# A hybrid decoder layer on one core: DeltaNet values turned in place by VectorE, outputs normed chunk by chunk and turned in halves

## The chip, the cores and the metric

The kernel runs on one NeuronCore of a Trainium2 chip. The core has TensorE (PE, matrix products, whose weight loads are listed as PEld), VectorE (DVE), ScalarE (ACT), GpSimd (POOL) and SyncE (SP), which here issues nearly all of the transfers; 16 DMA engines carry them. The engines run side by side, each through its own queue in order, and wait for each other by semaphores. The metric is the time of one execution on the device in microseconds; smaller is better.

## The reference, cut to what matters

The whole is one decoder layer for 1024 tokens of width 1024. One input projection feeds two mixers: a gated DeltaNet (4 heads of 128) and a dilated attention (8 heads of 64). Their outputs go through one output projection, a gated MLP of width 2816 with a short convolution follows, and a final norm. The change lies in the DeltaNet's values and outputs:

```python
qkv_a = silu(causal_dwconv(qkv_a, conv_qkv_w))       # width 4, per channel
qa = l2norm(qa) * 128**-0.5; ka = l2norm(ka)         # va as it is
# per chunk of 64 tokens: a triangular solve, then
def step(state, xs):
    uv, wk, qd, at, ke, ge = xs
    u = uv - wk @ state                              # uv comes from the values va
    o = qd @ state + at @ u
    state = ge * state + ke.T @ u
    return state, o
o_a = rmsnorm(o_a, gdn_norm_w) * silu(z)             # norm over the 128 features of a head
x = x + concat([o_a, o_b]) @ w_out
```

The kernel works with chunks of 128 tokens, of which there are eight (`NCH`).

## The kernel before, in words

Activations lie by feature: 128 features on the partitions, 1024 tokens along the free dimension. Weights and activations of the large products are split in a high and a low part (`split`: ACT makes the high part, DVE the remainder), and each product is three matrix products (`mm3`).

*Who sets the order.* The program is written as Python generators (streams) which a small planner, `Weave`, interleaves. It keeps a model time for PE and for the other engines (`Engine.account`: a fixed cost and a cost per element) and lets a stream go on when its tiles should be ready (`need`, with a slack in us that is added). The streams have levels: the recurrence (`chain`) goes ahead of the dense products (`dense`). The order that comes out is PE's order for good: every matrix product gets an order token. On the other engines a scheduler of the language orders the instructions by a simulated timeline and by priority; `uv` and `ua` are DVE and ACT with high priority, `ve` and `ac` without, `po_` is POOL, `sy` and `sq_` are transfers on SP's queue. `after(a, b)` puts a behind b on their engine. Line 140 is the call through which the instructions of normal priority go, line 142 the same for high priority, 193 a matrix product, 197 a transpose on PE and 202 a half-height one.

*The dense products.* `DENSE` lists 128-column blocks of the input projection in order: the last keys, two of the attention's blocks, then queries and values of heads 0 to 3 in turn, then the rest of the attention's blocks and the gates z. The first key blocks are made before. For each block `dense` splits the next weights (`wk`, `weight`) and fetches the ones after (`raw_weight`, tile `wst`); `conv_silu` makes the convolution on ACT and DVE, and the SiLU on ACT.

*Preparation of a head.* `kprep` turns keys to token order (`tokens`: eight PE transposes into PSUM, copied out by ACT), and makes decays and the matrices `um`. `qprep` does the queries and parks them in DRAM (`qpark`, `atpark`). `vprep` turns the values: eight PE transposes, and ACT copies each 128 x 128 block out of PSUM, scaled per token by `nk`, into `vtok`. After the last key, `forward_sub` inverts all 32 x 32 diagonal blocks on DVE in 31 steps; the result goes through DRAM (`xdram`, `xtdram`) and `merges` joins the blocks on PE to the inverse, in `um`. That 32 x 32 turning trick is also used for the attention's values: DVE turns each 32 x 32 block of a tile, and the transfers through DRAM (`avdram`) put the blocks in place.

*The recurrence.* `chain(h)`, one stream per head, waits until all merges and all values are done. Per chunk: two products with the state, `r` on DVE, a product with the inverse, `wke` on DVE and its copy `w` on ACT, the new state `ct` on DVE; then the output chunk, which replaces the value chunk in `vtok` (ACT, then DVE), and its sum of squares (`osq`, ACT, accumulated in a column of `ms`). Heads 2 and 3 run some chunks behind heads 0 and 1. PE fills its waits with dense products.

*The output of a head.* After the eighth chunk DVE makes mean plus EPS in `ms`, POOL raises all eight columns to the power -1/2 (`rsqrt`) and multiplies the whole `vtok` by them. `finish` then turns `vtok` back on DVE in four instructions of 128 x 256 (tile `ft`) and writes it to `mixer`. `dense` reads it back when it makes the gate z (tile `og`), again with the blocks put in place by the transfer. The tag of a tile names the ring of slots that it takes; `ft` takes one of the key slots.

Attention begins after the recurrence; its softmax uses ACT's Exp. The SiLU before and the Exp after lie in different function tables, so ACT loads a table in between.

## Time and profile before

| | |
|---|---|
| median of 3 runs | 1201.64 us (1201.17 to 1201.66) |
| the profiled execution | 1199.71 us, its span 1197.9 us |
| granted TensorE clock, mean | 0.998 |
| instructions | 18219 |
| PE busy | 1184.3 us, 99% |
| DVE / ACT / POOL busy | 967.5 / 566.4 / 54.3 us |

The profile is one execution. "Busy" counts the time in which an engine has at least one instruction under way. A group line gives line, engine, operation, output and inputs, shape and count, then busy time and mean nanoseconds of one instruction, then the idle time just before them and what ended it. A timeline line starts with start and duration in us; in brackets stands the idle time before it and who released it. `SPq` is a transfer's issue on SP's queue; the landing of the data is told apart. Spans on POOL are rough, and ends of matrix products are modelled, so that neighbours overlap in the list.

### The profile page before, as it was taken

How to read it: one execution, taken by the hardware profiler on the slowest of the kernel's cores; microseconds unless marked ns; L12 is line 12 of the kernel's file. 1: busy time of each engine (PE TensorE's matmuls, PEld its weight loads, DVE VectorE, ACT ScalarE, POOL GpSimd, SP SyncE). 2: the span in 40 equal slices, each digit the busy share in tenths (PEclk: the TensorE clock that was granted, in tenths of full speed). 3: DMA queues.
4: the chain of work that ended last, by engine and by line, in shares of the span. 5: the costliest groups of instructions: out<-in, count | busy, mean ns of one | idle time of the engine just before them, and what ended most of it. 6: DMA issues, size and time to landing. Idle time of an engine off the chain costs nothing.

```text
span 1197.9 us, 18219 instructions
## 1 busy us (share of the span) xinstructions
PE 1184.3 (99%) x6994; PEld 979.5 (82%) x6994; DVE 967.5 (81%) x1552; ACT 566.4 (47%) x1113; POOL 54.3 (5%) x50
## 2 busy tenths in 40 slices
PE   9999999998999999999999999999999999999997
PEld 7888888897777777888888888888888888888887
DVE  7686985586766687777898888989888889898987
ACT  7383344363433344555454544445444453445452
POOL 0212110023000000000000000000000000000001
PEclk9999999999999999999999999999999999999999
DMA  7423235536643314443222223131222396356724
GB/s 237 106 75 103 78 118 131 150 114 189 185 100 128 98 37 142 148 158 106 77 70 99 88 71 106 53 106 59 100 89 69 105 378 211 119 181 218 240 99 155
DMA packets 98600, 152.72 MB, mean 127 GB/s; under 512 B 37936, under 2 KB 51024, under 8 KB 98512
## 3 DMA queue, kind: packets, MB, share of 16 engines
q1 hardware_dynamic: 97792, 151.02, 39.4%
q8 instruction: 55, 0.90, 0.3%
q10 hardware_dynamic: 720, 0.53, 0.1%
q14 instruction: 33, 0.27, 0.1%
HBM read 115.59 MB, written 35.93 MB: 126 GB/s over the span
## 4 chain that ended last, share of the span: by engine, by line
PE 95%; DVE 2%; ACT 1%; issue 1%; DMA 1%; POOL 0%; DVEq 0%; ACTq 0%; POOLq 0%
PE ps L193 46%; PE pa L193 20%; PE dw L193 17%; PE pc L193 10%; PE ps L197 1%; PE ps L202 1%; DMA wst<-in_wu 1%; ACT sm L142 0%; PE warm L193 0%; DVE x1h L140 0%; DVE sm L142 0%; DVE aqkv L140 0%; DVE T L140 0%; ACT L142 0%; DVE wst L140 0%
## 5 line engine op out<-in xcount | busy, mean ns | idle before, releaser
L193 PE MATMUL dw<-pr 128*128 128x512 f32 (+1 forms) x984 | 211.4, 376 | 0.0
L193 PEld LDWEIGHTS dw<-pr 128*128 128x128 f32 x984 | 176.7, 188 | 33.7
L193 PE MATMUL ps<-xhi,whi 128*128 128x512 f32 x448 | 184.4, 412 | 0.0
L193 PE MATMUL ps<-xhi,wlo 128*128 128x512 f32 x448 | 175.2, 391 | 0.0
L193 PE MATMUL ps<-xlo,whi 128*128 128x512 f32 x448 | 174.8, 390 | 0.0
L193 PE MATMUL pa<-T,pair 128*128 128x512 f32 x528 | 127.1, 390 | 0.5 <-ACT u L140 0.5
L193 PEld LDWEIGHTS pa<-T,pair 128*128 128x128 f32 x528 | 98.9, 188 | 21.5 <-ACT u L140 1.0
L193 PEld LDWEIGHTS ps<-xhi,whi 128*128 128x128 f32 x448 | 84.3, 188 | 19.3 <-issue 2.7
L193 PEld LDWEIGHTS ps<-xhi,wlo 128*128 128x128 f32 x448 | 84.1, 188 | 18.5
L193 PEld LDWEIGHTS ps<-xlo,whi 128*128 128x128 f32 x448 | 84.4, 188 | 14.3
L140 ACT ACTIVATE u<-pa 128x512 f32<-128x512 f32 x44 | 26.3, 598 | 109.7 <-PE pa L193 109.7
L140 DVE SCALAR_TENSOR_TENSOR y<-xu,fcw,y 128x1023 f32<-128x1023 f32 (+1 forms) x44 | 56.4, 1281 | 24.4 <-ACT y L140 24.4
L140 ACT ACTIVATE whi<-wst 128x1024 fp32r<-128x1024 f32 (+2 forms) x38 | 38.5, 1014 | 68.8 <-PE ps L193 61.6
L140 ACT ACTIVATE pr<-wd 128x1024 fp32r<-128x1024 f32 x33 | 35.0, 1061 | 74.6 <-DVE wd L140 37.2
L193 PE MATMUL pa<-B,A 128*128 128x512 f32 x264 | 63.5, 389 | 0.0
L193 PE MATMUL pa<-T,S 128*128 128x512 f32 x264 | 63.4, 389 | 0.0
L193 PE MATMUL pc<-T,S 128*128 128x512 f32 x264 | 63.4, 389 | 0.0
L193 PE MATMUL pc<-B,pair 128*128 128x512 f32 x264 | 63.4, 389 | 0.0
L140 DVE TENSOR_TENSOR wst<-wst 128x512 f32<-128x512 f32 x88 | 60.4, 686 | 0.8
L193 PE MATMUL ps<-B,pair 128*128 128x512 f32 x252 | 60.5, 389 | 0.0
L142 ACT ACTIVATE sm<-sm,mx 128x128 f32<-128x128 f32 (+7 forms) x64 | 35.5, 555 | 50.3 <-DVE mx L142 50.3
L193 PEld LDWEIGHTS pc<-T,S 128*128 128x128 f32 x264 | 49.5, 188 | 10.3
(242 smaller groups left out, 2234.2 us busy)
## 6 DMA issues: line engine op xcount, KB each, us to landing
wst<-in_wu SPq DMA_DIRECT2D x44, 512.0 KB, 3.6
wd<-in_wd SPq DMA_DIRECT2D x44, 512.0 KB, 4.5
wst<-in_wi SPq DMA_DIRECT2D x25, 512.0 KB, 3.6
upark<-y SPq DMA_DIRECT2D x22, 512.0 KB, 3.5
r<-upark SPq DMA_DIRECT2D x22, 512.0 KB, 10.1
wa<-in_wd SPq DMA_DIRECT2D x22, 256.0 KB, 2.9
apark<-aqkv SPq DMA_DIRECT2D x8, 512.0 KB, 2.7
wst<-in_wo SPq DMA_DIRECT2D x8, 512.0 KB, 3.8
```

Of the source, the lines that this page charges most:

```text
L140: return getattr(eng, op)(*a, **kw)
L142: return getattr(eng, op)(*a, **kw)
L193: tc.stamp_issue_order_token(nc.tensor.matmul(dst, lhs, rhs, start=start, stop=stop, **kw).ins, TOKEN)
L197: tc.stamp_issue_order_token(nc.tensor.transpose(dst, src, ident).ins, TOKEN)
L202: tc.stamp_issue_order_token(nc.tensor.transpose(dst, src[rows], ident[rows, rows]).ins, TOKEN)
```

## The change

Five things change.

1. `vprep` makes no PE transposes any more. DVE turns the 32 x 32 blocks of the values' tile in place, four strided transfers write it to a new DRAM buffer `vdram`, one reads it back in token order as `vtok`, and ACT scales its eight blocks from SBUF. The planner waits for the tile with slack `VSLACK`, 3 us; the slack before the turning is 1 us instead of 3.
2. The output is normed by chunk: the square carries the factor 1/128 by its scale, POOL adds EPS and raises one column, and one chunk later ACT scales the chunk (`normed`).
3. The output is turned and written in halves (`half_turned`): the first four chunks at the fifth chunk of the recurrence, the others at the end. The halves take slots of the ring `t2`, which the planner charges to DVE by hand.
4. The weights of three blocks (`CHAINED`) are split in two halves of 512 columns.
5. After the last head's values ACT runs one Exp on a tile of one column (`mark`), ordered behind that head's SiLU.

```diff
+VSLACK = 3.0
+CHAINED = [("a", 1, 1), ("a", 1, 2), ("a", 2, 0)]
...
-    def weight(src, n=1024, st=None):
+    def weight(src, n=1024, st=None, parts=1):
...
-        lows_made.append(split(st, hi, lo))
+        for i in range(parts):
+            sl = slice(i * n // parts, (i + 1) * n // parts)
+            low = split(st[:, sl], hi[:, sl], lo[:, sl])
+        lows_made.append(low)
...
+    vdram = dp.tile([H, P, S], F32, name="vdram")
...
         if j // 4 != 1:
-            ac.activation(y, y, AF.Silu)
+            last["silu"] = ac.activation(y, y, AF.Silu)
...
-                nxt = wk(None, raw.pop())
+                nxt = wk(None, raw.pop(), 1 + (DENSE[i + 1] in CHAINED))
...
                 v = conv_silu(xr, 8 + h, "vT", "qa")
+                if h == H - 1:
+                    after(ac.activation(mark, mhalf[:, :1], AF.Exp), last["silu"], "the table changes once")
                 wv.add(4, vprep(h, v))
...
     def vprep(h, vT):
         yield from wv.until(("q", h))
-        yield wv.need(vT, slack=SLACK)
-        G[h]["vtok"] = yield from tokens(vT, A("vtok", ("dv", "dw")[h % 2]), G[h]["nk"])
+        yield wv.need(vT, slack=1.0)
+        vtok, nk = A("vtok", ("dv", "dw")[h % 2]), G[h]["nk"]
+        ve.transpose(vT, vT)
+        blocks = vdram[h].rearrange("(a t) (c b i) -> b t c a i", a=4, c=NCH, b=4)
+        for b in range(4):
+            sq_.dma_start(blocks[b], vT[32 * b:32 * b + 32].rearrange("t (c a i) -> t c a i", c=NCH, a=4))
+        sy.dma_start(vtok, vdram[h])
+        yield wv.need(vtok, slack=VSLACK)
+        for c in range(NCH):
+            cs = slice(c * P, (c + 1) * P)
+            ac.activation(vtok[:, cs], vtok[:, cs], AF.Copy, scale=nk[:, c:c + 1])
+        G[h]["vtok"] = vtok
         wv.done.add(("v", h))
...
-            ua.activation(osq, vtok[:, cs], AF.Square, accum_out=ms[:, c:c + 1])
+            ua.activation(osq, vtok[:, cs], AF.Square, scale=128.0 ** -0.5, accum_out=ms[:, c:c + 1])
+            po_.tensor_scalar(ms[:, c:c + 1], ms[:, c:c + 1], EPS, None, op0=OP.add)
+            rsqrt(ms[:, c:c + 1], ms[:, c:c + 1], 1)
+            if c:
+                normed(vtok, ms, c - 1)
+            if c == 4:
+                half_turned(h, vtok, 0)
             wv.done.add(("c", h, c))
 
-        uv.tensor_scalar(ms, ms, 1.0 / 128, EPS, op0=OP.mult, op1=OP.add)
-        rsqrt(ms, ms, NCH)
-        po_.tensor_tensor(v8(vtok), v8(vtok), ms[:, :, None].to_broadcast([P, NCH, P]), op=OP.mult)
-        wv.add(1, finish(h, vtok))
-
-    def finish(h, osb):
-        yield wv.need(osb, slack=FSLACK)
-        t = A("ft", "kT*")
-        by_feature, src = ...
-        for b in range(4):
-            ve.transpose(by_feature[:, b], src[:, b])
-            yield 0.4
-        sy.dma_start(mixer[h], t)
+        wv.add(1, finish(h, vtok, ms))
+
+    def normed(osb, ms, c):
+        cs = slice(c * P, (c + 1) * P)
+        wv.free["scalar"] = max(wv.free["scalar"], wv.pe) + 0.23
+        nc.scalar.activation(osb[:, cs], osb[:, cs], AF.Copy, scale=ms[:, c:c + 1])
+
+    def half_turned(h, osb, hh):
+        t = tile_(sp, [P, 512], F32, "ft", "t2", 2)
+        by_feature = t.rearrange("p (b c i) -> p c b i", b=4, c=4)
+        src = osb[:, half(hh)].rearrange("p (c b j) -> p c b j", c=4, b=4)
+        for c in (0, 2):
+            wv.free["vector"] = max(wv.free["vector"], wv.pe) + 0.34
+            nc.vector.transpose(by_feature[:, c:c + 2], src[:, c:c + 2])
+        sy.dma_start(mixer[h].rearrange("p (b c i) -> p b c i", b=4, c=NCH)[:, :, 4 * hh:4 * hh + 4],
+                     t.rearrange("p (b c i) -> p b c i", b=4, c=4))
+
+    def finish(h, osb, ms):
+        yield wv.need(ms, slack=FSLACK)
+        normed(osb, ms, NCH - 1)
+        half_turned(h, osb, 1)
         wv.done.add(("o", h))
```

5 lines of the change are left out of this document (2 added, 3 removed).

## The prediction

> **What bounds the kernel now.** I read the page's first part, the chain's shares, PE's waits, and then a table of stages.
>
> ```profile
> PE 1184.3 (99%) x6994; PEld 979.5 (82%) x6994; DVE 967.5 (81%) x1552; ACT 566.4 (47%) x1113; POOL 54.3 (5%) x50
> PE 95%; DVE 2%; ACT 1%; issue 1%; DMA 1%; POOL 0%; DVEq 0%; ACTq 0%; POOLq 0%
> PE ps L193 <- DVE ct L142: 1.6, 2, 1.2
> PE ps L193 <- ACT w L142: 1.4, 2, 1.0
> PE ps L202 <- DVE sm L142: 1.1, 1, 1.1
> 115.00:175.00 60.00, 60.00 (x306) 50.83 (x306) 55.22 (x122) 24.12 (x72) 8.10 (x3) 1.00 0.26 88
> 175.00:198.00 23.00, 23.00 (x119) 19.32 (x117) 14.19 (x22) 10.39 (x30) 4.50 (x3) 1.00 0.69 181
> 198.00:226.00 28.00, 28.00 (x522) 24.36 (x522) 12.11 (x17) 8.68 (x22) 0.36 (x2) 1.00 0.48 141
> 226.00:292.00 66.00, 62.95 (x419) 56.62 (x418) 47.76 (x136) 33.53 (x130) 12.43 (x10) 1.00 0.42 134
> 292.00:470.00 178.00, 176.53 (x1791) 135.67 (x1790) 129.15 (x345) 71.23 (x213) 7.15 (x10) 1.00 0.41 114
> ```
>
> TensorE carries 95% of the chain. The stage rows give the stretch, then busy time of PE, PEld, DVE, ACT and POOL, then clock, DMA share and GB/s. From 115 to 226 us, where the values are made, PE is never idle: what leaves PE there shortens the kernel, unless a wait takes its place. In the recurrence (226 to 292) PE idles 3.05 us, and to 470 another 1.47; waits can be won there, 4.5 us at most.
>
> **Part 1: 32 transposes leave TensorE.**
>
> ```profile
> L197 PE MATMUL ps<-ident,vT 128*128 128x128 f32 x32 | 4.2, 274 | 0.0
> 127.31 1.04 PE L197 MATMUL ps<-ident,vT 128*128 128x128 f32 x8
> 128.10 0.47 PE L193 MATMUL ps<-xhi,whi 128*128 128x512 f32 x1
> 128.42 0.39 PE L193 MATMUL ps<-xlo,whi 128*128 128x512 f32 x1
> 128.65 0.40 PE L193 MATMUL ps<-xhi,wlo 128*128 128x512 f32 x1
> ```
>
> Eight transposes of one head hold PE from 127.31 to 128.10, 0.79 us; the product behind them takes a step of 0.32 where the next takes 0.23. So 0.88 us a head, 3.5 us for four (bounds: 4 x 0.79 = 3.2, and the group's 4.2). I take **-3.5**.
>
> **Part 2: the detour of the values.** Per head it adds one DVE transpose, four strided writes and one read on SP's queue, and ACT scales from SBUF instead of PSUM. Nearest rows: the attention's own values take the same way (`avt`, `avdram`).
>
> ```profile
> L140 DVE STREAM_TRANSPOSE avt<-aqkv x4: 1245/1245/1246, 209.9 to 393.8; 128x1024 f32<-128x1024 f32 x4
> L140 SPq DMA_DIRECT2D avdram<-avt x16: 580/676/1854, 212.4 to 397.1; - x16
> DMA to landing us min/median/max: 2.7/3.4/4.9
> qT<-apark SPq DMA_DIRECT2D x4, 512.0 KB, 4.0
> 128.61 2.15 ACT L142 ACTIVATE vtok<-ps,nk 128x128 f32<-128x128 f32 x8
> 232.24 0.31 ACT L142 ACTIVATE osq<-vtok 128x128 f32<-128x128 f32 x1
> 196.99 1.06 ACT L140 ACTIVATE vT<-vT 128x1024 f32<-128x1024 f32 x1 [3.65 <-DVE vT L140]
> 225.53 1.05 PE L193 MATMUL ps<-vtok,um 128*128 128x128 f32 x8
> ```
>
> The last head decides. Its SiLU ends at 198.05; transpose 1.25, four issues of 0.68, landing 3.4, read 4.0, eight scalings of 0.31: 211.9 (with issues of 1.85 and a landing of 4.9: 218.1). PE first uses values at 225.53, or 222.0 once 3.5 us are gone. So 4 to 10 us of cover, made of the merges' products; I take 0. If it fails, each us late is one us of idle PE. ACT's scaling costs 8 x 0.31 = 2.5 at most against 2.15, beside 24.12 busy of 60: nothing.
>
> The first three heads stand ahead of something stricter. The forward substitution (31 steps on DVE) feeds, through DRAM, the merges' first products.
>
> ```profile
> 173.69 1.13 DVE L140 COPY mt<-xi 128x1024 f32<-128x1024 f32 x1
> 186.08 3.94 SPq L140 DMA_DIRECT2D um<-xtdram x8
> um<-xtdram SPq DMA_DIRECT2D x16, 32.0 KB, 1.9
> 198.13 2.21 PE L193 MATMUL ps<-x,um 32*32 32x32 f32 x128
> ```
>
> The last tile lands at 186.08 + 3.94 + 1.9 = 191.9 and is used at 198.13: 6.2 us of slack. Against it: PE arrives 3 x 0.88 = 2.6 earlier; DVE, 55.22 of 60 busy, gets 3 x 1.25 = 3.7 more, and its 4.8 idle may absorb it or not; SP may put the third head's five transfers first, 4 x 0.68 and one more of like price, 3.4. All together 9.7, so 3.5 of idle PE at worst, 0 at best. `Weave` charges the transpose and the transfers to its engines before it places the merges behind dense products, which pulls towards 0: **+0.5**. The same reckoning covers other waits on SP: the read of `vdram` waits for its own writes at the queue's head, and a weight load behind it comes up to 4.9 late, but weights are fetched a column ahead, against 48 products x 0.23 = 11 us a column.
>
> **Part 3: the recurrence and its outputs.** Per head, DVE's small scaling of `ms`, one POOL power of 8 columns and one POOL product over 1024 columns go; per chunk, POOL adds EPS and raises one column, and ACT scales 128 columns. The 16 transposes keep their size, but 8 now fall at the fifth chunk. Mixer writes go from 4 to 8 of half size.
>
> ```profile
> 268.67 1.06 DVE L140 TENSOR_TENSOR aqkv<-ps,rstdB 128x512 f32<-128x512 f32 x1
> 269.64 1.90 POOL L140 TENSOR_TENSOR vtok<-vtok,ms 128x1024 f32<-128x1024 f32 x1
> 269.90 0.32 DVE L142 TENSOR_SCALAR wke<-ps,ke 128x128 f32<-128x128 f32 x1
> 270.38 2.23 DVE L140 TENSOR_TENSOR wlo<-wst,whi 128x1024 fp32r<-128x1024 f32 x1
> 270.58 0.49 PE L193 MATMUL ps<-wke,ktok 128*128 128x128 f32 x2 [0.98 <-ACT w L142]
> 272.93 0.49 PE L193 MATMUL ps<-ct,kT 128*128 128x128 f32 x2 [1.19 <-DVE ct L142]
> L140 DVE STREAM_TRANSPOSE ft<-vtok x16: 397/407/459, 267.4 to 299.0; 128x256 f32<-128x256 f32 x16
> L140 DVE TENSOR_TENSOR wlo<-wst,whi 128x1024 fp32r<-128x1024 f32 x33 | 41.2, 1250 | 5.0 <-ACT whi L140 4.9
> 292.60 1.64 POOL L140 TENSOR_TENSOR ms<-ms,mhalf 128x8 f32<-128x8 f32 x1 [0.91 <-DVE ms L142]
> 208.90 0.18 POOL L140 COPY mark<-x 1x1 f32<-1x1 f32 x1 [12.68 <-DVE x L140]
> L140 DVE SCALAR_TENSOR_TENSOR og<-og,gw,zz x4: 1274/1277/1285, 425.1 to 469.1; 128x1024 f32<-128x1024 f32 x4
> ```
>
> Gain: the state `ct` of one head stood behind a weight subtraction of 2.23 us (mean 1.25; POOL's 1.90 us product ran beside it), and PE waited 1.19. POOL's product goes, and the halves are about 0.63 each, so `ct` can slip between them: **-1.2** (0 if the two halves are issued in a row). The 0.98 wait for `w` goes back to `wke` behind DVE's 1.06 `aqkv` and transposes; fewer transposes at a head's end: **-0.5**.
>
> Loss: 32 scalings of up to 0.31 us enter ACT's queue, 9.9 us on 33.53 of 66, and each can stand ahead of a `w`. Bounds 0 and +9.9. ACT caused 1.4 us of waits; scaled by its load (43.4 / 33.5) that is 1.8, +0.4; DVE's transposes in mid-recurrence, 8 x 0.41, can hold a `ct` too, bounds 0 and 3.3. Together **+1.0**, near the row of today's waits, since a third of ACT stays free and `Weave` charges 0.23 for each. POOL's 64 small operations lie between 0.18 and 1.64 each; only the scaling one chunk later needs them: 0. If one came late, the scaling would stop ACT's queue with the next `w` behind it; that is in the bound of 9.9. The mixer's four more writes, 0.68 each on SP, are read back as `og` and first used at 425.1, over 100 us after the recurrence: 0.
>
> The splitting in parts adds three instruction starts on each of ACT and DVE: nothing while PE has its weights a column ahead.
>
> **Part 4: the table.**
>
> ```profile
> 293.31 1.28 ACT L142 ACT_TABLE_LOAD   x1 [1.00 <-DVE mx L142]
> 297.90 0.60 PE L202 MATMUL ps<-ident,sm 64*128 64x64 f32 x8 [1.08 <-DVE sm L142]
> ```
>
> The load stands before the first softmax, whose transposes PE then awaits 1.08 us. It moves behind the last head's SiLU, where ACT is busy 8.68 of 28 us and PE has the merges and dense products; 1.28 us there are covered by ACT's free 19. **-1.1** (0 if what is late next, `aqkv` on DVE, keeps it).
>
> **Sum:** -3.5 + 0.5 - 1.2 - 0.5 + 1.0 - 1.1 = **-4.8 us** on the profiled execution's 1199.71 (span 1197.9): 1194.9. That execution lies 1.93 below the runs' median, 1201.64, from which I predict **1196.8 us**, 0.4% faster. About 0.2%, 2.4 us, is what a measurement of this kernel tells from no change: below 1199.2 is faster, above 1204.0 slower.
>
> [...] Beside POOL's 1.90 us product, DVE's subtraction took 2.23 instead of 1.25. [...]
>
> **Rivals.**
> 1. *Slower: ACT's queue in the recurrence.* If a `w` or a `vtok` waits behind a scaling in PE's fixed order, each costs up to 0.31. The other terms give -5.8, so 19 uncovered scalings of 32 cancel the gain, and all 32 give 1201.64 - 5.8 + 9.9 = 1205.7. For it: 226 to 292 holds most of PE's idle time before 470. Against: ACT is busy 51% there and would be 66%. Chance 0.14.
> 2. *The forward substitution is late.* All 9.7 add up: +3.5 instead of +0.5, 1199.8, at the bound of "same". For: DVE has only 4.8 us free of 60. Against: the planner's order. Chance 0.13.
> 3. *DVE locked out by small POOL operations.* 64 of at least 0.18 hold 11.5 us; if half of that reaches PE through `ct` and `wke`, +5.8: 1202.6, same. Against: today's eight hold 4 x (1.64 + 1.90) = 14.2 in longer pieces, and DVE is free 18 us of 66. Chance 0.05.
> 4. *The 3.5 us move into a later wait* (attention loses that much dense work to fill with): 1200.3, same. Against: PE idles only 1.47 us from 292 to 470, with work left over. Chance 0.01.
>
> **Chances and range.** Forecast (1193 to 1199): 0.67. Faster: 0.67 and 0.08 of rival 2, 0.75. Slower: rival 1 and part of 3, 0.16. Same: the rest, 0.09. Range: below, all of 4.2 and all 4.5 us of waits go, 1192.9; above, rival 1 up to two thirds of its price, 1201.64 - 5.8 + 6.6 = 1202.4, which takes in rivals 2 and 4 and most of 3. The forecast's own range is 1193.5 to 1199.
>
> **What would show it.** No `ident,vT` group, 3.5 us less PE busy time; `ps<-x,um` and the first `vtok,um` without idle before them; no table load near the first softmax; no wait of PE near 1 us for `ct` or `w`. Wrong if PE's idle time from 226 to 292 rises above 3.05 with ACT as releaser, or if PE idles before the merges.

## The result, and the profile after

The changed kernel takes 1212.26 us (median; 1209.52 to 1214.92), the kernel before, run beside it, 1201.41 us: a ratio of 1.0087, 95% interval 1.0071 to 1.0102. It is 0.9% slower. The prediction was 1196.8 us with a range up to 1202.4: the sign is wrong, and the time lies 10 us outside the range. One slow execution of a later kernel (query_first, 3048.06 us against the 1211 to 1212 of its others) is left out of its ratio.

The profiled execution takes 1209.52 us (span 1207.7) against 1199.71 (1197.9) before. From the page of the changed kernel, the busy times, the chain's shares by engine, and four of TensorE's waits (engine, line, tile, whom it waited for: us in total, times, longest):

```profile
PE 1187.3 (98%) x6962; PEld 978.6 (81%) x6962; DVE 969.1 (80%) x1555; ACT 578.0 (48%) x1149; POOL 66.4 (6%) x106
PE 87%; DVE 5%; DMA 3%; ACT 2%; issue 1%; SPq 1%; POOL 0%; DVEq 0%; ACTq 0%; POOLq 0%
...
PE ps L197 <- DVE ct L146: 3.0, 4, 1.9
PE ps L201 <- ACT qT L144: 2.8, 2, 2.2
PE ps L206 <- DVE sm L146: 2.5, 4, 1.3
PE ps L197 <- ACT w L146: 1.8, 4, 1.0
```

TensorE's share of the chain falls from 95% to 87%; transfers, VectorE and ScalarE have moved onto it. The same stages as in the prediction's table:

```profile
115.00:175.00 60.00, 59.41 (x295) 49.93 (x294) 54.93 (x115) 24.44 (x72) 6.17 (x3) 1.00 0.41 115
175.00:198.00 23.00, 20.81 (x91) 16.95 (x90) 14.87 (x24) 10.59 (x30) 4.05 (x3) 0.93 0.66 165
198.00:226.00 28.00, 27.89 (x521) 24.11 (x520) 14.79 (x26) 10.66 (x25) 0.86 (x3) 1.00 0.81 201
226.00:292.00 66.00, 61.18 (x383) 53.47 (x382) 41.95 (x126) 38.49 (x145) 23.69 (x58) 0.97 0.47 149
292.00:470.00 178.00, 174.52 (x1792) 134.51 (x1792) 124.75 (x347) 70.26 (x225) 7.67 (x18) 1.00 0.36 106
```

Before, PE had no idle time from 115 to 226 us; now it has 0.59 + 2.19 + 0.11 there, 4.82 where it had 3.05, and 3.48 where it had 1.47. And the granted clock is below 1.00 in two of these stages, and in none of them before.

From all of PE's rows in the two executions (the step from the start of one product to the start of the next, less idle time), the 9.8 us of the span come out so: idle time +6.8 (6.5 to 13.3), the transposes that are gone -3.2, two stretches of half clock +3.4, and +2.8 in the steps of other products, some 1.9 of it at products just before or behind a wait, which don't overlap their neighbour there (the one at 188.45 holds PE for 0.39 us where the step is 0.23).

Where it begins is in ScalarE's waits between 115 and 310 us and in the timeline of 160 to 236 us (start, duration; in brackets the idle time before it and its releaser):

```profile
ACT vtok L144 <- DMA vtok<-vdram: 28.1, 4, 8.9
```

```profile
181.30 1.12 DVE L144 COPY mt<-xi 128x1024 f32<-128x1024 f32 x1
182.67 0.37 SPq L144 DMA_DIRECT2D xdram<-xi  x1
187.58 2.45 ACT L144 ACTIVATE vtok<-vtok,nk 128x128 f32<-128x128 f32 x8 [8.88 <-DMA vtok<-vdram]
189.93 1.04 ACT L144 ACTIVATE qT<-qT 128x1024 f32<-128x1024 f32 x1
191.03 1.29 PE L201 MATMUL ps<-ident,qT 128*128 128x128 f32 x8 [2.19 <-ACT qT L144]
199.44 4.98 SPq L144 DMA_DIRECT2D um<-xtdram  x8
...
218.45 2.45 ACT L144 ACTIVATE vtok<-vtok,nk 128x128 f32<-128x128 f32 x8 [5.66 <-DMA vtok<-vdram]
230.57 0.83 PE L197 MATMUL ps<-vtok,um 128*128 128x128 f32 x6
235.37 0.38 PE L197 MATMUL ps<-vtok,um 128*128 128x128 f32 x2
```

For each of four heads ScalarE stands still until the transposed values have come back from DRAM, 28.1 us in all. What is queued behind the scaling waits with it: at 189.93 the next head's queries, for which TensorE idles 2.19 us. The forward substitution ends late on VectorE (the copy behind it starts at 181.30, 173.69 before), its result goes to DRAM at 182.67 (173.73 before), behind the read of `vdram` on SP's queue, and its last tiles are loaded from 199.44 on (186.08 before). The last head's values are scaled at 218.45 to 220.9, and the first products of the recurrence stand at 230.57 (six) and, behind 15 dense products, at 235.37 (two), where all eight stood at 225.53 before.

### The profile page after: what moved, and what is told of

Its sections match the earlier page's. It is cut to its first block, busy times and chain, and to the rows that moved or that the text cites. A ratio compares the mean times of both kernels' runs of the same rounds, so it can differ in the third digit from the quotient of the medians.

```text
span 1207.7 us, 18310 instructions
## 1 busy us (share of the span) xinstructions
PE 1187.3 (98%) x6962; PEld 978.6 (81%) x6962; DVE 969.1 (80%) x1555; ACT 578.0 (48%) x1149; POOL 66.4 (6%) x106
## 4 chain that ended last, share of the span: by engine, by line
PE 87%; DVE 5%; DMA 3%; ACT 2%; issue 1%; SPq 1%; POOL 0%; DVEq 0%; ACTq 0%; POOLq 0%
PE ps L197 39%; PE pa L197 19%; PE dw L197 17%; PE pc L197 10%; PE ps L206 1%; DMA vdram<-vT 1%; DMA mixer<-ft 1%; SPq L144 1%; DVE vT L144 1%; PE ps L201 1%; ACT sm L146 1%; DMA xdram<-xi 1%; DMA wst<-in_wu 0%; DVE wlo L144 0%; DVE sm L146 0%
## 5 line engine op out<-in xcount | busy, mean ns | idle before, releaser
L144 ACT ACTIVATE whi<-wst 128x1024 fp32r<-128x1024 f32 (+3 forms) x41 | 38.8, 952 | 60.4 <-PE ps L197 52.6
L197 PE MATMUL ps<-B,pair 128*128 128x512 f32 x252 | 60.5, 389 | 0.0
```

What stands on the lines that cost most here:

```text
L144: return getattr(eng, op)(*a, **kw)
L197: tc.stamp_issue_order_token(nc.tensor.matmul(dst, lhs, rhs, start=start, stop=stop, **kw).ins, TOKEN)
```

## The experiments

The first table gathers what the runs and their profiles gave. "Ratio" is to the kernel before, with its 95% interval. The next columns come from the profiled execution of each: the start of the first `vtok,um` product (the recurrence begins), the first and the last `r,um` product and the stretch between them (seven steps of four heads), the number of dense products that the planner put into this stretch (0.23 us each), VectorE's idle time right before output transposes (`ft`), and the time lost to half clock (the sum over 1 us windows of one less the granted clock, without the last 8 us, where every execution has some).

| kernel | ratio | vtok,um | r,um | stretch | dense in it | before ft | half clock |
|---|---|---|---|---|---|---|---|
| before | 1 | 225.5 | 233.7 to 289.0 | 55.3 | 90 | 0.9 | 0 |
| changed | 1.0087 (1.0071 to 1.0102) | 230.6 | 242.2 to 302.7 | 60.5 | 84 | 7.1 | 3.4 |
| values_only | 1.0033 (1.0020 to 1.0046) | 235.6 | 247.2 to 302.6 | 55.4 | 87 | 0.3 | 5.1 |
| outputs_only | 1.0019 (1.0009 to 1.0028) | 226.0 | 234.1 to 294.2 | 60.1 | 87 | 7.0 | 1.7 |
| no_detour | 1.0020 (1.0011 to 1.0029) | 226.5 | 234.7 to 295.3 | 60.6 | 87 | 7.3 | 1.7 |
| table_chained | 0.9999 (0.9990 to 1.0007) | 226.2 | 234.3 to 289.7 | 55.4 | 90 | 0.9 | 1.7 |
| query_first | 1.0084 (1.0067 to 1.0101) | 232.3 | 243.9 to 304.5 | 60.6 | 84 | 7.7 | 6.8 |
| detour_last | 1.0072 (1.0057 to 1.0087) | 231.0 | 242.7 to 304.0 | 61.3 | 84 | 8.1 | 3.4 |
| last_in_step | 1.0015 (1.0004 to 1.0026) | 226.3 | 234.4 to 295.7 | 61.3 | 102 | 8.6 | 1.7 |
| all_told | 1.0062 (1.0045 to 1.0078) | 231.7 | 239.9 to 301.6 | 61.7 | 90 | 7.5 | 5.1 |
| last_values | 1.0013 (1.0003 to 1.0023) | 228.6 | 236.7 to 292.9 | 56.2 | 93 | 2.4 | 1.7 |
| ring_of_three | 1.0055 (1.0039 to 1.0072) | 232.9 | 244.6 to 300.6 | 56.0 | 84 | 3.8 | 3.4 |
| no_detour_ring | 1.0017 (1.0008 to 1.0027) | 226.5 | 234.7 to 294.2 | 59.5 | 87 | 6.0 | 3.4 |
| normed_only | 1.0032 (1.0020 to 1.0045) | 226.3 | 234.4 to 295.5 | 61.1 | 114 | 1.6 | 1.7 |
| no_detour_split | 1.0028 (1.0019 to 1.0037) | 225.6 | 233.8 to 292.3 | 58.5 | 87 | 7.3 | 0 |
| factors_only | 1.0020 (1.0010 to 1.0029) | 226.1 | 234.2 to 289.4 | 55.2 | 90 | 0.2 | 1.7 |
| scaled_at_end | 1.0049 (1.0037 to 1.0061) | 225.4 | 233.6 to 297.6 | 64.0 | 114 | 2.5 | 3.4 |
| normed_by_pool | 1.0031 (1.0020 to 1.0042) | 226.3 | 234.4 to 293.8 | 59.4 | 90 | 2.8 | 3.4 |
| split_by_pool | 1.0022 (1.0014 to 1.0031) | 226.2 | 234.4 to 295.0 | 60.6 | 96 | 6.6 | 0 |

(The row of query_first has its profile from query_first_again, the same kernel.)

### Which part costs

The changed kernel with the old `vprep`, and the kernel before with one part alone.

no_detour:

```diff
-        yield wv.need(vT, slack=1.0)
-        vtok, nk = A("vtok", ("dv", "dw")[h % 2]), G[h]["nk"]
-        ve.transpose(vT, vT)
...
-        G[h]["vtok"] = vtok
+        yield wv.need(vT, slack=SLACK)
+        G[h]["vtok"] = yield from tokens(vT, A("vtok", ("dv", "dw")[h % 2]), G[h]["nk"])
```

> The changed kernel without the values' detour: outputs by chunk and in halves, weights in halves, table early. outputs_only was at 1203.9; the early table should take about 1 us and the halves of the weights up to 1: 1202 to 1203. If these two do nothing: 1204.

values_only (the kernel before, with the new `vprep` and `vdram`) and outputs_only (the kernel before, with the norming by chunk, `normed`, `half_turned` and the new `finish`):

> The kernel before with the values' detour alone. Theory A: -3.5 us of transposes, +2.8 of waits for qT, +1.6 of lower clock, +0.5 of pipeline drains: about 1203. Rival B (the detour is harmless and the outputs cost everything): 1198.

> The kernel before with the outputs' part alone (normed by chunk, turned in halves, written in halves). Theory B: TensorE waits for ct and wke behind DVE's transposes that wait for a slot of t2 (4.2 us in the changed kernel's DVE waits), and the clock drops once; 1205 to 1209. If only ACT's queue before the recurrence counts (theory A alone): 1200 to 1202.

table_chained (the kernel before, with the early table load and the `CHAINED` halves):

> The kernel before with two parts of the change alone: the ScalarE table load moved behind the last head's values, and the three weight columns split in halves. By the prediction's terms, -1.1 for the table and -1.7 for the halves (1.2 of ct behind wlo, 0.5 of w): 1198.6 to 1200.5. Rival: the waits of the recurrence come back elsewhere and only the table's 1.1 stays, or nothing: 1200.3 to 1201.5.

Measured: values alone 1205.11 us, outputs alone 1203.93, table and halves alone 1199.92 against 1200.21 before. In ratios +0.33%, +0.19% and -0.01%; the whole change has +0.87%. values_only came out 2 us above the sum of theory A, outputs_only between its two ranges; table_chained lies in the theory's range in us, but only because the kernel before ran at 1200.21 us beside it. So each of the two large parts costs by itself, and 0.36%, some 4 us, seem to come only together; by the four intervals that is anything from 0.1 to 0.6%. Without the detour 0.20% is left, so the detour, on top of the rest, costs 0.67%, 8 us.

The small parts gave nothing, and the trace of table_chained says why. First the two halves of the weights, then the softmax that lost its table load:

```profile
271.00 2.30 DVE L142 TENSOR_TENSOR wlo<-wst,whi 128x512 fp32r<-128x512 f32 x2
273.22 0.34 DVE L144 SCALAR_TENSOR_TENSOR ct<-ct,ge,ps 128x128 f32<-128x128 f32 x1
273.61 0.49 PE L195 MATMUL ps<-ct,kT 128*128 128x128 f32 x2 [1.26 <-DVE ct L144]
...
295.01 1.90 POOL L142 TENSOR_TENSOR vtok<-vtok,ms 128x1024 f32<-128x1024 f32 x1
295.14 2.04 DVE L144 TENSOR_SCALAR sm<-sm,mx 128x128 f32<-128x128 f32 x2
298.60 0.60 PE L204 MATMUL ps<-ident,sm 64*128 64x64 f32 x8 [1.08 <-DVE sm L144]
```

The halves stand in a row (x2, 2.30 us beside the 2.23 of the whole), `ct` behind both, and PE waits 1.26 us where it waited 1.19. And without the table load VectorE's softmax scaling comes earlier, 0.13 us after the start of GpSimd's product of 1.90 us, where it came 1.42 us after it; there its two instructions take 2.04 us instead of 0.77, and PE waits the same 1.08 us. In the kernel before:

```profile
295.73 0.77 DVE L142 TENSOR_SCALAR sm<-sm,mx 128x128 f32<-128x128 f32 x2
```

In both the first of the two ends 0.1 us after the product, and in table_chained the second 0.3 us after it.

### The detour: ScalarE's queue

query_first orders the scalings of a head behind the next head's query SiLU. query_first_again is the same kernel; its trace is the one read below.

```diff
-            last["silu"] = ac.activation(y, y, AF.Silu)
+            last["silu"] = silus[j] = ac.activation(y, y, AF.Silu)
...
-            ac.activation(vtok[:, cs], vtok[:, cs], AF.Copy, scale=nk[:, c:c + 1])
+            inst = ac.activation(vtok[:, cs], vtok[:, cs], AF.Copy, scale=nk[:, c:c + 1])
+            if h < H - 1:
+                after(inst, silus[h + 1], "the next queries go first")
```

> The changed kernel with one thing added: each head's eight scalings of the values are ordered on ACT behind the SiLU of the next head's queries. Theory A (ACT's queue: the scaling waits for its transfer, 28.1 us in four waits, and the next queries' SiLU stands behind it): the two waits of TensorE for qT (0.59 and 2.19 us) go, and the stretch at a granted clock of 0.68 behind the second goes with them (1.6 us); 5 us less than the changed kernel's 1212, about 1207. Rival B (the recurrence's outputs are at fault): the qT waits go and come back as a wait before the merges; 1211 to 1213.

> The same program as query_first, for a profile of it. Theory A' (the forward substitution is late by itself: 6.5 us of DVE and then SP's queue and the transfers): TensorE's waits for qT are gone, and it waits 1.5 to 5 us for the merges' operands x and um instead, near 200 us; the time is 1211 to 1212. Theory A (ACT's queue alone): no wait there, and the time lost stands in the recurrence.

Measured: 1212.03 us, ratio 1.0084 (1213.59 us in the one run of query_first_again): nothing gained. Of the trace of query_first_again, one of ScalarE's waits, and two groups of TensorE:

```profile
ACT vtok L144 <- DMA vtok<-vdram: 4.7, 4, 2.9
```

```profile
198.58 0.21 PE L197 MATMUL ps<-x,um 32*32 32x32 f32 x2 [2.82 <-DMA x<-xdram]
199.84 1.91 PE L197 MATMUL ps<-x,um 32*32 32x32 f32 x62 [1.05 <-DMA x<-xdram]
```

ScalarE's wait shrinks from 28.1 to 4.7 us and TensorE no longer waits for queries. It then waits 3.87 us for the merges' tiles instead: the forward substitution is late by itself (its result goes out at 181.64, against 173.73 before). In the changed kernel TensorE does not wait for these tiles; there the wait for the queries comes first. The queue on ScalarE is a real wait, but another stands right behind it.

### The detour: who holds the recurrence

detour_last gives the first three heads the old transposes back and leaves the detour to the last head.

```diff
+        if h < H - 1:
+            yield wv.need(vT, slack=SLACK)
+            G[h]["vtok"] = yield from tokens(vT, A("vtok", ("dv", "dw")[h % 2]), G[h]["nk"])
+            wv.done.add(("v", h))
+            return
```

> The changed kernel, but heads 0 to 2 turn their values on TensorE as before; only the last head takes the detour. Theory A': the forward substitution ends on DVE near 173.7 us again, xdram is written near 174, there is no wait for qT, and 2.6 of the 3.5 us of transposes are back: 1206 to 1208. Rival (the last head's transfers make the recurrence late by themselves): above 1210.

Measured: 1210.52 us, ratio 1.0072. The forward substitution is back in time (its result goes out at 174.00), and the waits for queries are gone; yet the first `vtok,um` product still stands at 231.0. The last head's detour does that alone.

last_in_step is detour_last with one edit more: it tells the planner that these values are done when their transfers have been issued.

```diff
         sy.dma_start(vtok, vdram[h])
-        yield wv.need(vtok, slack=VSLACK)
-        for c in range(NCH):
-            cs = slice(c * P, (c + 1) * P)
-            ac.activation(vtok[:, cs], vtok[:, cs], AF.Copy, scale=nk[:, c:c + 1])
         G[h]["vtok"] = vtok
         wv.done.add(("v", h))
...
             qT, at = [qa[:, i, (c % 4) * P:(c % 4 + 1) * P] for i in range(2)]
+            if h == H - 1:
+                ua.activation(vtok[:, cs], vtok[:, cs], AF.Copy, scale=d["nk"][:, c:c + 1])
```

> As detour_last (1210.52; heads 0 to 2 turned by TensorE as before, the last head by the detour), but the planner is told that the last head's values are done when their transfers are issued, and the scaling of each of their eight chunks is issued inside the recurrence, just ahead of its first use. Theory: the last head's transfers land in time (its scalings ended at 212.9 in detour_last), and what cost the 7 us between no_detour (1203.63) and detour_last was the planner, which held all four recurrences for those values and laid a whole dense column ahead of them that was then missing as cover. Then the first vtok,um product goes back to 225 to 227, and the time is that of no_detour within the eight scalings (8 x 0.31 on ScalarE in the recurrence) and the eight transposes saved (about 0.9): 1202.5 to 1206. Rival: the transfers and the VectorE transpose themselves cost it, through the queue of SyncE and what is queued behind them: 1208 or above, whatever the planner was told.

Measured: 1202.53 us, ratio 1.0015. The timelines of detour_last and of last_in_step:

```profile
210.86 2.45 ACT L144 ACTIVATE vtok<-vtok,nk 128x128 f32<-128x128 f32 x8 [3.00 <-DMA vtok<-vdram]
231.03 0.83 PE L197 MATMUL ps<-vtok,um 128*128 128x128 f32 x6
235.83 0.38 PE L197 MATMUL ps<-vtok,um 128*128 128x128 f32 x2
```

```profile
210.40 2.45 ACT L146 ACTIVATE vtok<-vtok,nk 128x128 f32<-128x128 f32 x8 [2.35 <-DMA vtok<-vdram]
226.29 1.05 PE L197 MATMUL ps<-vtok,um 128*128 128x128 f32 x8
```

In both, ScalarE scales the last head's values in a row at 210 to 213 us (in last_in_step they are issued in the recurrence with high priority, and were moved up to that place). The same work at the same time, 0.57% or some 7 us apart: the data were never late. What differs is the order that `Weave` wrote. `chain` of every head waits until all heads have `("v", i)`; with the detour's transfers and `VSLACK` charged, that comes later by the planner's reckoning, and it lays dense products ahead of the recurrence. In the trace, 774 of them stand before the first `vtok,um` in detour_last, 762 in last_in_step (759 before), and 813 against 786 (783) before the first `r,um`: 27 more, 6.2 of the 8.2 us by which this comes later. Between the first and the last `r,um` there are 84 instead of 102 in a stretch of the same length: the recurrence starts late and has less work to fill its waits.

all_told does the same to the whole changed kernel, all four heads by the detour.

> The changed kernel whole, all four heads by the detour, with the one edit of last_in_step: the planner is told that the last head's values are done when their transfers are issued, and their scalings stand in the recurrence. Theory: the losses of the detour add up from two places, the late forward substitution (TensorE's waits for qT and x between 160 and 200 us, some 4 us with the lower clock after them) and the planner's hold of the recurrence for the last head's values (some 7 to 8 us). Then this edit gives back the second alone: 1204 to 1208. Rival: the two are one loss, since the late merges would hold the recurrence anyway: 1209 or above, with the first vtok,um product still at 230.

Measured: 1207.75 us, ratio 1.0062. It gives back 0.25%, 3 us (by the two intervals 0.2% more or less), where I expected 4 to 8: the time is inside what was said, the first `vtok,um` (231.7) is where the rival put it. The timeline shows where the two losses meet:

```profile
205.36 3.63 SPq L144 DMA_DIRECT2D vdram<-vT  x3
220.13 2.45 ACT L146 ACTIVATE vtok<-vtok,nk 128x128 f32<-128x128 f32 x8 [7.35 <-DMA vtok<-vdram]
222.61 1.08 ACT L144 ACTIVATE x<-ps 64x512 f32<-64x512 f32 x2
223.25 2.04 PE L197 MATMUL ps<-um,x 64*64 64x64 f32 x29 [1.35 <-ACT x L144]
```

With the forward substitution late, its tile loads hold SP's queue up to 204.8, so the last head's transfers start at 205.36 (200.55 in last_in_step), the values come at 220 instead of 210, and ScalarE, 7.35 us in that wait, lets the merges' copies stand behind it. So the losses overlap: the hold costs 7 us where the forward substitution is in time and 3 us where it is late.

last_values is the kernel before with the last head's detour alone, told early.

> The kernel before with the values part alone, for the last head alone, and the planner told early as in last_in_step; outputs, table and weights as before. Theory: with the hold gone, eight transposes less on TensorE are a gain (0.9 us of steps in last_in_step), and the eight scalings on ScalarE cost less than that: a ratio of 0.9985 to 0.9998 to the kernel before. Rival: the scalings inside the recurrence cost as much as the transposes saved: 1.000 to 1.001.

Measured: 1201.78 us, ratio 1.0013 (1.0003 to 1.0023), a little above the rival's range and not by its mechanism: eight transposes leave TensorE (0.85 us of steps), but PE waits 0.96 us for the merges' `um`, where it waited for nothing before, and a stretch of half clock (1.7 us) follows. Over all runs the granted clock, 0.9960 against 0.9973 of the kernel before beside it, is 1.5 us by the span, an estimate, and so the whole of the loss. Even without the hold the detour is no gain.

### The outputs: the shared buffer

In outputs_only one wait stands out. VectorE, ScalarE and TensorE in its timeline:

```profile
278.07 0.77 DVE L893 STREAM_TRANSPOSE ft<-vtok 128x256 f32<-128x256 f32 x2 [3.67 <-DMA mixer<-ft]
278.77 0.31 DVE L142 TENSOR_SCALAR wke<-ps,ke 128x128 f32<-128x128 f32 x1
279.11 0.28 ACT L142 ACTIVATE w<-ps 128x128 f32<-128x128 f32 x1 [3.50 <-DVE wke L142]
279.44 0.80 PE L193 MATMUL ps<-wke,ktok 128*128 128x128 f32 x2 [3.40 <-ACT w L142]
```

A half-turn waits for a free buffer of the ring `t2` (two slots), that is, for an earlier half's write to land. The recurrence's `wke` stands behind it in VectorE's queue, ScalarE's `w` waits with it, and TensorE idles 3.40 us. ring_of_three and no_detour_ring give that ring three slots, for all its users, in the changed kernel and in no_detour:

```diff
-        t = tile_(sp, [P, 512], F32, "ft", "t2", 2)
+        t = tile_(sp, [P, 512], F32, "ft", "t2", 3)
...
```

> The changed kernel with three slots instead of two in the ring t2, from which the halves come. Theory B: DVE's three waits for the mixer's writes (4.2 us) shrink to under 1 us, and TensorE's waits for ct and wke at 284 to 295 us (3.6 us) with the clock's drop behind them (1.7 us); 1207 to 1209. If the wait for the slot only stands where DVE would be idle anyway: 1211 to 1213.

> no_detour with three slots in the ring t2. Theory B: the waits of TensorE behind DVE's wait for a slot (2.0 and 3.4 us in outputs_only) go: 1198 to 1200, faster than the kernel before. If they come back as other waits in the recurrence: 1202 to 1203.

Measured: 1208.56 us (1.0055) and 1203.26 us (1.0017). In the changed kernel VectorE's waits for a write disappear, the stretch falls from 60.5 to 56.0 and 0.32% comes back (by the two intervals 0.2% more or less). Without the detour one such wait of 2.6 us remains, the stretch stays at 59.5, and nothing comes back. So the buffer is a cause in the one order of work and not in the other.

no_detour_split keeps the halves apart (second halves into a buffer of the head's own), and normed_only undoes the half-turns altogether:

```diff
-        t = tile_(sp, [P, 512], F32, "ft", "t2", 2)
+        t = A("ft", "kT*")[:, :512] if hh else tile_(sp, [P, 512], F32, "ft", "t2", 3)
...
```

> As no_detour (1203.63), still turned in halves, but no half has to wait for another's write: the ring of the first halves has three buffers, and the second halves go into the head's own buffer that the kernel before used. Theory (the wait for the buffer): DVE's wait for mixer<-ft goes from 4.7 us to under 1, TensorE's idles of 2.58 and 3.34 us go, and the time is 1198 to 1201. Rival (turning in the middle of the recurrence costs by its place in VectorE's order, not by the buffer): 1202.5 to 1204.

```diff
             if c:
                 normed(vtok, ms, c - 1)
-            if c == 4:
-                half_turned(h, vtok, 0)
...
         normed(osb, ms, NCH - 1)
-        half_turned(h, osb, 1)
+        t = A("ft", "kT*")
...
+        for b in range(4):
+            ve.transpose(by_feature[:, b], src[:, b])
+            yield 0.4
+        sy.dma_start(mixer[h], t)
```

> As no_detour (1203.63), but the outputs, normed chunk by chunk by ScalarE as in the changed kernel, are turned and written as in the kernel before: four transposes of a head at its end, into a buffer of the head's own, one write. Theory: what the outputs part costs is the half-turns, whose buffer (a ring of two, shared by all heads) VectorE waits for until a write to mixer has landed (4.7 us in no_detour, of which 3.6 at one place, where the TensorE idles of 2.58 and 3.34 us follow); then these waits go, and the time is 1198 to 1201. Rival: it is the norming by chunk itself, 32 scalings on ScalarE and 64 small operations more on GpSimd in the recurrence: 1202.5 to 1205.

Measured: 1204.06 us (1.0028) and 1204.59 us (1.0032). The theory of the buffer missed in both: it said 1198 to 1201. In no_detour_split one wait of 3.1 us for a write remains, so it is a weak test; normed_only has none, turns where the kernel before turned, and is no faster. Its stretch of 61.1 us is no loss, though: it holds 24 dense products more than before, 5.5 of the 5.8 us. TensorE's idle time from 226 to 292 us is even less than before (2.16 against 3.05), from there to 600 us it is more (3.83 against 2.00), a stretch of half clock costs 1.7, and 2.5 us are spread over the steps of many products. So what normed_only loses does not stand in the recurrence, and its cause is open.

### The outputs: who scales

factors_only and scaled_at_end take the two new pieces apart, each in the kernel before:

```diff
-            ua.activation(osq, vtok[:, cs], AF.Square, accum_out=ms[:, c:c + 1])
+            ua.activation(osq, vtok[:, cs], AF.Square, scale=128.0 ** -0.5, accum_out=ms[:, c:c + 1])
+            po_.tensor_scalar(ms[:, c:c + 1], ms[:, c:c + 1], EPS, None, op0=OP.add)
+            rsqrt(ms[:, c:c + 1], ms[:, c:c + 1], 1)
...
-        uv.tensor_scalar(ms, ms, 1.0 / 128, EPS, op0=OP.mult, op1=OP.add)
-        rsqrt(ms, ms, NCH)
```

> The kernel before with one piece of the outputs part: the factor of each chunk (one addition and one power on GpSimd behind its square) is made in the recurrence, 64 small operations, while the scaling by it stays one GpSimd multiplication of the whole head, and the turning and the writing stay as they were. If the outputs part costs by the small GpSimd operations (their access to memory beside VectorE's, the prediction's third rival): 1.002 to 1.003. If it costs by ScalarE's 32 scalings, which this kernel has not: 0.9995 to 1.0008.

```diff
-        po_.tensor_tensor(v8(vtok), v8(vtok), ms[:, :, None].to_broadcast([P, NCH, P]), op=OP.mult)
+        for c in range(NCH):
+            cs = slice(c * P, (c + 1) * P)
+            ac.activation(vtok[:, cs], vtok[:, cs], AF.Copy, scale=ms[:, c:c + 1])
```

> The other piece: the factors made at once at a head's end as in the kernel before, but applied by eight ScalarE scalings instead of GpSimd's one multiplication; turned and written as before. If ScalarE's scalings cost by their time in its queue wherever they stand: 1.001 to 1.003. If they cost only because each stands in the recurrence's order behind a factor that is not there yet (the waits of ScalarE for ms, 8 to 10 us in the kernels with norming by chunk): 0.999 to 1.0005.

Measured: 1202.84 us (1.0020) and 1205.82 us (1.0049). The ratio of factors_only is the one named for GpSimd's small operations, but its trace doesn't bear that out: the stretch is 55.2 us, as before, and VectorE is not slowed in it. Its loss comes later: the last head's output is ready sooner, its four transposes (1.40 us) slip ahead of the softmax's scaling, PE waits 2.16 us there instead of 1.08, and a stretch of half clock (1.7 us) follows. Over all its runs the granted clock, 0.9957 against 0.9973 beside it, is 1.9 of the 2.4 us by the span, an estimate. scaled_at_end has the longest stretch of all, 64.0, but 5.5 of the 8.7 us more are dense products (114 for 90). In its timeline, one head's scalings and what follows:

```profile
265.28 2.45 ACT L140 ACTIVATE vtok<-vtok,ms 128x128 f32<-128x128 f32 x8 [0.73 <-POOL ms L140]
270.61 0.57 PE L193 MATMUL ps<-ct,qat 128*128 128x128 f32 x2 [2.72 <-DVE vtok L142]
```

Eight scalings in a row hold ScalarE's queue for 2.45 us, with the other heads' `vtok` behind them; the `vtok` on VectorE, which TensorE awaits, stands in addition behind VectorE's transposes and a weight subtraction.

normed_by_pool and split_by_pool take the scalings off ScalarE, in normed_only and in no_detour_split:

```diff
-        wv.free["scalar"] = max(wv.free["scalar"], wv.pe) + 0.23
-        nc.scalar.activation(osb[:, cs], osb[:, cs], AF.Copy, scale=ms[:, c:c + 1])
+        wv.free["gpsimd"] = max(wv.free.get("gpsimd", 0.0), wv.pe) + 0.42
+        nc.gpsimd.tensor_scalar(osb[:, cs], osb[:, cs], ms[:, c:c + 1], None, op0=OP.mult)
```

> As normed_only (1204.59, ratio 1.0032: normed chunk by chunk, turned and written at a head's end as before), but the 32 scalings are done by GpSimd, which has made their factors, and no longer stand in ScalarE's queue. Theory (ScalarE's queue): the stretch from the first r,um product to the last, 55.3 us in the kernel before, 55.2 with the factors alone, 61.1 in normed_only and 64.0 in scaled_at_end, comes back to 55 to 57, and the ratio to 0.999 to 1.001. Rival (GpSimd's work between VectorE's, or the longer way to the outputs): the stretch stays above 59, the ratio at 1.002 or above.

> As no_detour_split (1204.06, ratio 1.0028: table, halves of weights, norming by chunk, turned in halves without a shared buffer), with the 32 scalings on GpSimd. Theory: as in normed_by_pool, the stretch of 58.5 comes back to 55 to 57; with the table load gone from the first softmax, 0.998 to 1.0005, the best that is left of the change. Rival: the half-turns in mid-recurrence keep it at 1.0015 or above.

Measured: 1204.35 us (1.0031) and 1203.03 us (1.0022), as slow as with ScalarE; the stretches are 59.4 and 60.6. ScalarE's queue is not the whole of it. In normed_by_pool:

```profile
270.13 1.42 DVE L144 STREAM_TRANSPOSE ft<-vtok 128x256 f32<-128x256 f32 x4 [2.77 <-POOL vtok L893]
272.58 0.32 DVE L146 TENSOR_SCALAR wke<-ps,ke 128x128 f32<-128x128 f32 x1
272.94 0.28 ACT L146 ACTIVATE w<-ps 128x128 f32<-128x128 f32 x1 [0.71 <-DVE wke L146]
273.27 0.79 PE L197 MATMUL ps<-wke,ktok 128*128 128x128 f32 x2 [2.91 <-ACT w L146]
```

It is the picture of outputs_only again, with another name in the bracket. There VectorE's transposes waited for a write, here for GpSimd's scaling; in both the recurrence's small operations stand behind them, and TensorE waits about 3 us. To compare the stretches in the table, take off 0.23 us for each dense product above 90 and add it for each below. Then the kernels in which VectorE idles up to 2.4 us before `ft` have 55.2 to 56.1 us, those with 2.5 to 3.8 have 57.4 to 59.4, and those with 6.0 or more have 58.6 to 62.7. So the wait before the transposes goes with the length of the recurrence, but this is an order among 19 executions and no test, and it is not the whole loss: normed_only loses 0.32% with 55.6 us. What is left open is how much each engine's queue has of it. The traces suggest a cause in the code: `half_turned` issues its transposes with no `wv.need` at all, and `finish` waits for `ms`, not for the scaled chunk. To wait for the chunk there was not tried.

No kernel of the study beats the kernel before by more than its interval; table_chained (0.9999) is level with it.

## Why the prediction was wrong

**Part 1, the transposes (-3.5): right.** There is no `ident,vT` group any more, and the steps of PE's rows that go with it are 3.23 us.

**Part 2, the cover of the last head (taken as 0): wrong, by some 7 us where the rest is in time.** The step said that the values, ready at 211.9, are wanted at 222.0, and that "each us late is one us of idle PE". In detour_last they were scaled by 213.3, so the estimate of the data was good. It failed because the start of the recurrence is not set by the data but by the planner's reckoning of them: it held `chain` and put 27 more dense products ahead of the first `r,um`. PE did not idle for the values before those products (0.83 us for the merges' `um` at 216.0, with a stretch of half clock behind it, is its only wait there); the price was paid later, in detour_last mostly between 285 and 313 us (5.8 us of idle time and 1.7 of half clock), where the recurrence and the first softmax lack cover. The prediction did name that `Weave` charges the transfers, and took it for a help. (In the whole changed kernel the values did come late as well, at 220.9, behind the um loads on SP.)

**Part 2, the forward substitution (+0.5): wrong size, rival 2's mechanism.** The terms were 2.6 + 3.7 + 3.4 = 9.7 us of lateness against 6.2 of slack, taken near zero. Measured: the result goes to DRAM 8.9 us later (173.73 to 182.67). VectorE has 6.5 of it, where the step allowed 3.7 for the transposes and left it open whether free time absorbs them; the rest is the wait behind the read of `vdram` on SP's queue. The idle time that it leaves, freed of the queries' wait, is 3.87 us (query_first_again), the 3.5 of the bound, with 3.4 us of half clock behind it. In the changed kernel itself the queries' wait stands ahead of it, and PE does not idle there.

**Part 2, ScalarE (0): wrong.** The step costed the scaling's duration, 2.45 against 2.15 us, and not its wait. Each scaling waits in ScalarE's queue until a round trip through DRAM has ended (28.1 us in four), and the next head's query SiLU is queued behind it: 2.8 us of idle PE. In the trace VectorE is done with the last head's queries at 183.61 (182.33 + 1.28), and their SiLU starts at 189.93, behind the scaling that had waited 8.88 us.

**Part 3, the gain (-1.7): not in the sum.** In table_chained, with GpSimd's product still there, the halves are issued in a row: the bound of 0 that I named and did not take. In no_detour, without that product, `ct` does slip between two halves, as the step had it:

```profile
266.50 0.65 DVE L144 TENSOR_TENSOR wlo<-wst,whi 128x512 fp32r<-128x512 f32 x1
267.07 0.34 DVE L146 SCALAR_TENSOR_TENSOR ct<-ct,ge,ps 128x128 f32<-128x128 f32 x1
267.33 0.68 DVE L144 TENSOR_TENSOR wlo<-wst,whi 128x512 fp32r<-128x512 f32 x1
```

But 2.58 us of PE's idle time for `vtok` and 3.34 for `w` follow at 268 and 280. The wait for `w`, which was to shrink by 0.5 with fewer transposes at a head's end, became the 3.40 us of outputs_only: fewer transposes stand there, but they wait.

**Part 3, the loss (+1.0): too small.** outputs_only costs 0.19%, 2.3 us, without the gains. The scaling took 400 ns a piece, not 310:

```profile
L905 ACT ACTIVATE vtok<-vtok,ms 128x128 f32<-128x128 f32 x32 | 12.8, 400 | 6.6 <-POOL ms L144 6.3
DVE ft L913 <- DMA mixer<-ft: 4.2, 3, 2.1
```

The half-turns were costed by their own 8 x 0.41 us and not by what they wait for: in the changed kernel 4.2 us for writes and 2.9 for the scaling, with the recurrence's `ct`, `wke` and `r` behind them. The buffer, a ring of two for the halves of four heads where a head took a `kT*` buffer before, was not in the sum at all. Rival 1 (ScalarE's queue) has its mechanism seen in the timeline of scaled_at_end, but not as the only one: with the scalings on GpSimd the loss stays (normed_by_pool). Rival 3 (VectorE held by small GpSimd operations) was an estimate whose one row, 2.23 us instead of 1.25, stands beside a long product of 1.90 us; no run shows such a hold for the small ones, and it falls: factors_only has all 64 and a stretch of 55.2 us.

**Part 4, the table (-1.1): the load moved** (it stands at 198.12 in the changed kernel), **the gain did not come** while GpSimd's product is there (table_chained). In no_detour, where that product is gone too, the wait at the first softmax is gone; but the time is lost before it.

**The sum.** In hundredths of a per cent of 1201 us: values alone +33, outputs alone +19, table and halves -1, and +36 that come only together. No term of the prediction stood for that. A reason would be that the detour moves dense work ahead of the recurrence, and the outputs' waits need just that work as cover; but this is not shown. In the profiled executions nothing is left over: the parts alone take 7.4, 4.2 and 2.1 us more than the kernel before, the whole 9.8 (single executions; that of values_only is the slowest of its runs, that of the changed kernel the fastest). Nor did a term stand for the clock, which the prediction took as full: half clock is 3.4 of the 9.8 us.

## What to carry to other kernels

When an instruction that waits for a transfer is put on a busy engine, price the wait and list what is queued behind it; its own duration was the least of it here (2.45 us a head, against 28.1 us of waits in four). Where a planner writes the order, ask what it will do with the new due time: data that are in time on the chip can still move a whole stage, and the price is paid later, where cover is missing. A gate that all heads pass together (here `("v", i)` of all four) makes one late head everybody's.

## What I had not expected of the hardware

After some of the short waits TensorE's granted clock was 0.50, in these executions always for 3.41 us or twice that, which costs 1.71 us for each 3.41 (the last 8 us of an execution left out). In the changed kernel, behind the wait of 2.19 us, a dense product takes a step of 0.43 us where it takes 0.23 at full clock (1 us windows; the clock is the number after the last bracket):

```profile
191.00:192.00 1.00, 0.97 (x9) 0.98 (x9) 0.05 (x1) 1.00 (x2) 0.13 (x1) 0.90 0.72 115
192.00:193.00 1.00, 1.00 (x5) 0.81 (x4) 1.00 (x1) 1.00 (x2) 0.00 (x0) 0.50 0.85 134
...
195.00:196.00 1.00, 1.00 (x5) 0.77 (x5) 1.00 (x3) 0.00 (x0) 0.15 (x1) 0.90 0.41 65
```

The losses in the last column of the table are multiples of it: 0, 1.7, 3.4, 5.1, 6.8. It followed idle times of 0.83 us (detour_last) to 3.40 us (outputs_only), but not each: in all_told PE idled 3.23 us up to 274.1 and went on at full clock:

```profile
273.00:274.00 1.00, 0.00 (x0) 0.00 (x0) 1.00 (x3) 0.00 (x0) 0.00 (x0) 1.00 0.94 356
275.00:276.00 1.00, 1.00 (x8) 0.91 (x7) 0.89 (x4) 0.74 (x3) 0.83 (x3) 1.00 0.65 188
```

The traces show more than chance in this. Two stretches of one execution start a whole number of 3.413 us apart: 191.79 and 287.37 in the changed kernel (28.0 times), 203.34 and 575.39 in ring_of_three (109.0 times). From such starts I estimate a raster of 3.413 us; against the kernel's start it lies differently in the two, 0.7 us past a whole number of steps in the changed kernel and 2.0 in ring_of_three. Lay it over PE's idle time from 100 to 600 us in the 19 executions: each of the 13 steps of the raster with 2.0 us or more of idle time was followed by half clock, and of the 29 with 1 to 1.92 us only four were, all beside the small products of the merges or the transposes of a softmax. The 3.23 us of all_told fall into two steps, as 1.75 + 1.48, and no_detour_split's 2.58 as 1.6 + 1.0; neither was followed by half clock. Below 1 us it came eight times, three of them beside the merges' small products and five between 566 and 579 us. Why it followed some of the shorter idle times and not others is not shown.

So in these executions 2.0 us or more of idle time within one step of the raster cost itself and at least 1.7 us more, and 1 to 1.92 us did so four times in 29. The half clock also goes with part of the scatter between runs of one kernel: table_chained, last_in_step, normed_only, no_detour_ring and ring_of_three have such a stretch between 566 and 579 us, in work that no experiment touched, and the kernel before in its profiled execution has none. Of the kernel before, 43 runs at a mean granted clock of 0.998 have a median of 1199.71 us, 29 runs at 0.996 one of 1201.69.
